# A decoder layer in float32: the second hidden tile of each FFN goes through seven block products

## The chip, the core and the metric

The kernel runs on one core of a Trainium2 chip. The core has a matrix engine (TensorE, PE in the profile, its weight loads PEld), a vector engine (VectorE, DVE), an activation engine (ScalarE, ACT), a general engine (GpSimd, POOL) and a queue engine (SyncE, SP) that issues the DMAs. Each engine works through its own list of instructions in order, and waits on semaphores for the others. The metric is the device time of one execution in microseconds.

## The reference

One layer of a decoder on 1024 tokens of width 1024, all in float32. Two SwiGLU feed-forward networks (FFNs) with a hidden width of 2816 stand at its two ends, and two attentions between them:

```python
def swiglu(x, w_gate, w_up, w_down):
    return (jax.nn.silu(x @ w_gate) * (x @ w_up)) @ w_down

x = x + 0.5 * swiglu(rms_norm(x, ffn1_norm), ffn1_w_gate, ffn1_w_up, ffn1_w_down)
# h = rms_norm(x) @ w_in, two causal attentions, gates, w_o
x = x + 0.5 * swiglu(rms_norm(x, ffn2_norm), ffn2_w_gate, ffn2_w_up, ffn2_w_down)
```

Only `x @ w_gate` and `x @ w_up` of the two FFNs are touched here.

## The kernel before, in words

**Splitting.** Each float32 operand is split into a rounded high part and a rest. ACT casts the high part, DVE subtracts it from the operand (`split_sb`, L157 to L160). A product is then three matmuls: high by high, high by low, low by high.

**Tiles.** The hidden width of 2816 is cut into 22 tiles of 128. Tokens stand in two halves of 512 (n = 0 and 1). For a tile, gate and up have to be computed for both halves of the tokens, over 8 blocks of 128 of the input width.

**A plain tile** takes two outputs, two halves, 8 blocks and 3 matmuls of 128x512: 96 matmuls. In the first FFN tile 0 is begun while the normalisation of the later tokens still runs (`first_half`, L267); the second half of the tokens follows in `ffn_up` (L464). Tile 1 is plain too: its weights are split whole (`col_split`, L434 and L435, 128x1024 each) and `proj_T` does the work (L501 to L506).

**A tile by seven products.** Gate and up, with the input width halved, are the four blocks of a 2x2 matrix, and so are the tokens. Seven products of sums of blocks give the four results (Strassen's scheme in Winograd's form). Each product is 4 blocks of 128 and 3 matmuls, so a tile is 84 matmuls. What it needs beside them:

- the sums of tokens t1 to t4, made once for each FFN (`token_sums`, L533): DVE adds and subtracts whole 128x1024 or 128x2048 pieces (L558, L564, L568, L572, L573), then ACT and DVE split them;
- for each tile the sums of weights, four POOL instructions of 128x512 (`pair_sums`, L596, L597, L598, L609), and seven splits of 128x512 (names `op`), ACT's cast and DVE's subtraction each;
- the adding up in `hidden_tile` (L625): three products share one PSUM bank (`pst`, a), and between them ACT and DVE copy or add what stands in it (L643, L648, L652, L655, L658, L662, L668); the bank may be added to again only when it has been read. The last product of a tile is emitted inside the next tile (`last`, called there as `finish`).

The weights of tile j are loaded two tiles ahead (`pair_load`, L581). The POOL sums of a tile take a buffer of the ring `y`, which has two buffers and is also that of tile 0's two results `a0` (L487). These are written out to DRAM from it (L492).

**Down projection.** `ffn_down` (L675) multiplies by w_down; tiles 2 to 21 go through seven products there as well, from sums that POOL makes of pairs of tiles (`act_sums`, L522). Tiles 0 and 1 are multiplied plainly at its end from `actd`.

**Order.** The order on each engine is set when the program is built, by the order of the Python calls and by the scheduler of the framework; nothing reorders at run time. The stretch that matters here is the beginning of each `ffn_up`: tile 0's second half, the token sums, and tiles 1 and 2.

Of the kernel before, what the change touches and what calls it, by code (L numbers as in the profile page):

```python
# [9 lines left out]
F32 = mybir.dt.float32  # L10
# [3 lines left out]
AF = mybir.ActivationFunctionType  # L14
ALU = mybir.AluOpType
AX = mybir.AxisListType

P = 128
T = 1024
# [4 lines left out]
NH = HID // P  # L24
# [39 lines left out]
class Layer:  # L64
# [399 lines left out]
    def ffn_up(self, norm, name, first, tags):  # L464

        nc = self.nc  # L470
        hi, lo = norm["hi"], norm["lo"]
        hT = hi, lo
        dst, sumd = self.actd[name == "ffn2"], self.sumd[name == "ffn2"]
        sums = norm["ops"]
        even = None
        blocks, (pg, pu) = first
        loads = {j: self.pair_load(name, j, tags["w"]) for j in (2, 3)}
        for n in range(2):
            s = slice(n * HALF, (n + 1) * HALF)
            if n == 1:  # L480
                pg, pu = self.psbg(), self.psbg()
                for o, w in zip((pg, pu), blocks):
                    self.high(o, w, hi[1])
                for o, w in zip((pg, pu), blocks):
                    for f in self.low(o, w, hi[1], lo[1]):
                        f()
            a = self.ring.tile([P, HALF], F32, tag="y", bufs=2, name="a0")  # L487
            nc.scalar.activation(a, pg, AF.Silu)
            if n == 0:
                self.follow(self.last_act)  # L490
            nc.vector.tensor_tensor(out=a, in0=a, in1=pu, op=ALU.mult)
            nc.sync.dma_start(dst[0][:, s], a)  # L492
            sums[1](n)
            if n == 0:
                sums[3](1)
        nxt = self.pair_sums(loads.pop(2))
        sums[2]()
        bg, bu = (self.col_split(l) for l in self.ffn_loads(name, 1))
        sums[4]()
        tok = sums["all"]()  # L500
        pg = self.proj_T(bg, hT)  # L501
        a = self.ring.tile([P, T], F32, tag="y", bufs=2, name="a")
        nc.scalar.activation(a, pg, AF.Silu)
        pu = self.proj_T(bu, hT)
        nc.vector.tensor_tensor(out=a, in0=a, in1=pu, op=ALU.mult)
        nc.sync.dma_start(dst[1], a)  # L506
        ops = [next(nxt) for _ in range(7)]
        finish = None
        for j in range(2, NH):
            if j + 2 < NH:  # L510
                loads[j + 2] = self.pair_load(name, j + 2, tags["w"])
            nxt = self.pair_sums(loads.pop(j + 1)) if j + 1 < NH else iter(())
            e = self.slot(tags["e"][j % 3]).rearrange("p (s n) -> p s n", s=4)
            then = None
            if j % 2:
                then = lambda a=even, b=e, k=j // 2 - 1: self.act_sums(a, b, sumd[:, :, k, :])
            ops, finish = self.hidden_tile(ops, tok, e, nxt, finish, then if j < NH - 1 else None)
            even = e
        finish()
        return then  # L520
# [1075 lines left out]
```

## Time and profile before

| what | value |
|---|---|
| median of 3 runs | 2150.81 us (2148.9 to 2152.93) |
| the profiled execution | 2152.22 us, of it 2150.1 us span from first to last instruction |
| granted TensorE clock | 1.000 |
| PE busy | 2107.7 us (98%) |
| DVE busy | 1323.2 us (62%) |
| ACT busy | 948.4 us (44%) |
| POOL busy | 711.5 us (33%) |

A row of a timeline reads: start in us, duration in us, engine, line, operation, output tile <- input tiles, shapes, count, and in brackets how long the engine was idle before it and what released it. Names leave out buffer numbers: `op` is a split weight operand of the seven products, `s_u`, `s_v`, `s_act`, `s_wd` are the big buffers that hold tokens, weights or results in turn, `psa`, `psb`, `psg`, `pst` are PSUM banks. A row with a count shows the time from the first start to the last end.

### The profile page before, as it was taken

Reading aid. Unit: us, or ns where it says so; the run is one execution under the profiler, and the core shown is the slowest. Engines: PE = TensorE matmul, PEld = TensorE weight load, DVE = VectorE, ACT = ScalarE, POOL = GpSimd, SP = SyncE. Lnnn points to the kernel's source line nnn. Section 1 sums busy time; section 2 is a strip of 40 time slices with the busy share of each in tenths; the row PEclk is TensorE's granted clock in tenths of the full one; section 3 lists DMA queues with packets and bytes.
Section 4 is the critical chain, followed back from the end, with each engine's and each line's share of the span. In section 5 each row is a group of like instructions: output and inputs, shape, how many; then the busy total and the mean of one; then the engine's idle time right before and its main releaser. Section 6 shows DMA issues by size and latency. Waiting matters only on the chain.

```text
span 2150.1 us, 27820 instructions
## 1 busy us (share of the span) xinstructions
PE 2107.7 (98%) x10113; PEld 1758.7 (82%) x10113; DVE 1323.2 (62%) x2140; ACT 948.4 (44%) x1758; POOL 711.5 (33%) x633
## 2 busy tenths in 40 slices
PE   7999999999999989999999999999999999999999
PEld 6888888878888767888888878888888888887887
DVE  7644444467766787645556677753844444449765
ACT  6333333334444544356656765422533333334441
POOL 0565555572201130023333432000354545546200
PEclk9999999999999999999999999999999999999999
DMA  5143332485334376675555774541232434266432
GB/s 172 54 138 98 110 116 89 137 301 173 113 109 148 94 214 194 204 188 138 138 144 139 183 210 126 197 166 65 83 98 79 137 98 135 81 228 239 133 106 107
DMA packets 251633, 305.37 MB, mean 142 GB/s; under 512 B 17656, under 2 KB 186472, under 8 KB 251496
## 3 DMA queue, kind: packets, MB, share of 16 engines
q1 hardware_dynamic: 251496, 303.59, 45.5%
q8 instruction: 80, 1.31, 0.3%
q14 instruction: 57, 0.47, 0.1%
HBM read 205.54 MB, written 98.00 MB: 141 GB/s over the span
## 4 chain that ended last, share of the span: by engine, by line
PE 86%; DVE 4%; issue 3%; DMA 3%; ACT 2%; SPq 1%; POOL 1%; ACTq 0%; POOLq 0%; DVEq 0%
PE pst L620 20%; PE psd L760 16%; PE psb L620 11%; PE psg L620 4%; PE pss L1379 4%; PE pspt L1405 3%; PE pspv L1416 3%; PE psgate L153 2%; PE psgate L155 2%; PE psgate L154 2%; PE psb L153 2%; PE psb L154 2%; PE psb L155 2%; PE psin L153 1%; PE psin L154 1%
## 5 line engine op out<-in xcount | busy, mean ns | idle before, releaser
L760 PE MATMUL psd<-op 128*128 128x512 f32 x1680 | 381.9, 389 | 1.4 <-DVE op L160 1.4
L760 PEld LDWEIGHTS psd<-op 128*128 128x128 f32 x1680 | 315.2, 188 | 67.7 <-DVE op L160 2.3
L160 DVE TENSOR_TENSOR op<-s_u,op 128x512 fp32r<-128x512 f32 x220 | 200.0, 912 | 111.5 <-ACT op L159 111.0
L159 ACT CAST op<-s_u 128x512 fp32r<-128x512 f32 x220 | 136.0, 621 | 214.3 <-PE psd L760 94.1
L620 PE MATMUL pst<-s_u,op 128*128 128x512 f32 x720 | 173.1, 389 | 0.8 <-DVE s_wd L662 0.8
L620 PE MATMUL pst<-s_v,op 128*128 128x512 f32 x640 | 167.9, 389 | 2.8 <-DVE s_u L662 2.8
L160 DVE TENSOR_TENSOR op<-s_act,op 128x512 fp32r<-128x512 f32 x125 | 114.4, 917 | 77.5 <-ACT op L159 77.1
L620 PEld LDWEIGHTS pst<-s_u,op 128*128 128x128 f32 x720 | 135.1, 188 | 29.2 <-DVE s_wd L662 1.2
L620 PEld LDWEIGHTS pst<-s_v,op 128*128 128x128 f32 x640 | 120.1, 188 | 28.2 <-DVE s_u L662 3.3
L1386 ACT ACTIVATE s_act<-pss,nm 128x128 f32<-128x128 f32 (+7 forms) x128 | 94.9, 742 | 100.8 <-DVE nm L1383 100.4
L596 POOL TENSOR_TENSOR sums<-s_u 128x512 f32<-128x512 f32 x20 | 28.0, 1402 | 320.1 <-DVE wlo L435 176.4
L159 ACT CAST op<-s_act 128x512 fp32r<-128x512 f32 x125 | 77.5, 622 | 110.7 <-PE pst L620 55.6
L160 DVE TENSOR_TENSOR op<-sums,op 128x512 fp32r<-128x512 f32 x80 | 60.0, 751 | 86.6 <-ACT op L159 86.1
L1379 PE MATMUL pss<-s_wd 96*128 96x256 f32 (+5 forms) x480 | 112.8, 361 | 0.0
L160 DVE TENSOR_TENSOR op<-s_wd,op 128x512 fp32r<-128x512 f32 x95 | 84.1, 890 | 38.5 <-ACT op L159 38.5
L1424 DVE TENSOR_TENSOR cmb<-pspv,cmb 64x512 f32<-64x512 f32 x64 | 44.1, 688 | 103.5 <-ACT cmb L1423 103.1
L155 PE MATMUL psgate<-s_u,wlo 128*128 128x512 f32 x256 | 100.7, 393 | 1.7 <-POOL wlo L435 1.7
L153 PE MATMUL psgate<-s_u,whi 128*128 128x512 f32 x256 | 101.6, 397 | 0.4 <-ACT z L1228 0.4
L1409 DVE TENSOR_TENSOR s_v<-pspt,s_v 128x512 fp32r<-128x512 f32 (+1 forms) x160 | 96.4, 632 | 7.4 <-ACT s_v L1408 5.8
L154 PE MATMUL psgate<-s_u,whi 128*128 128x512 f32 x256 | 100.7, 393 | 0.0
L159 ACT CAST op<-s_wd 128x512 fp32r<-128x512 f32 x95 | 58.4, 620 | 92.2 <-PE psd L760 89.1
L435 POOL TENSOR_TENSOR wlo<-stg,whi 128x1024 fp32r<-128x1024 f32 x19 | 45.4, 2394 | 160.8 <-DMA mk<-mlo 104.5
(507 smaller groups left out, 4894.0 us busy)
## 6 DMA issues: line engine op xcount, KB each, us to landing
sumd<-s_u SPq DMA_DIRECT2D x20, 1024.0 KB, 4.2
sumd<-s_wd SPq DMA_DIRECT2D x13, 1024.0 KB
s_wd<-fd SPq DMA_DIRECT2D x48, 256.0 KB, 5.4
s_u<-in_ffn_w_down_dram SPq DMA_DIRECT2D x22, 512.0 KB, 6.2
s_wd<-sumd SPq DMA_DIRECT2D x14, 768.0 KB, 4.3
s_u<-sumd SPq DMA_DIRECT2D x14, 768.0 KB, 4.3
s_act<-in_ffn_w_gate_dram SPq DMA_DIRECT2D x20, 512.0 KB, 4.1
s_act<-in_ffn_w_up_dram SPq DMA_DIRECT2D x20, 512.0 KB
```

Source lines behind the costliest of these rows:

```text
L153: mm(out, lhsT=lh, rhs=rh, start=start, stop=False)
L154: mm(out, lhsT=lh, rhs=rl, start=False, stop=False)
L155: mm(out, lhsT=ll, rhs=rh, start=False, stop=stop)
L159: self.nc.scalar.copy(hi, src)
L160: self.nc.vector.tensor_tensor(out=lo, in0=src, in1=hi, op=ALU.subtract)
L620: mm(out, lhsT=a[:, k, :], rhs=b[:, k, :], start=start and k == 0 and i == 0, stop=k == n - 1 and i == 2, skip_group_check=True,)
L760: nc.tensor.matmul(o, lhsT=u[:, r], rhs=w, start=start and m == 0, stop=k == CK - 1 and m == 2, skip_group_check=True,)
L1379: mm(ps[:, b:e], lhsT=a[:, q], rhs=bb[:, b:e], start=k == 0, stop=k == len(passes) - 1)
L1386: nc.scalar.activation(pn[:, :n], ps[:, :n], AF.Exp, bias=nm, accum_out=rs[:, i, j:j + 1])
L1405: nc.tensor.transpose(pt[:, o:o + P], pr[m][:, kt * P:(kt + 1) * P], self.ident)
L1409: nc.vector.tensor_tensor(out=lo, in0=pt[:, s0:], in1=hi, op=ALU.subtract)
L1416: mm(po[:, :256], lhsT=v[:, kt, :], rhs=slabs[c // 2][:, s, c % 2, e * 256:(e + 1) * 256], start=kt == 0 and s == 0, stop=False,)
```

## The change

Tile 1 of each FFN goes through `pair_load`, `pair_sums` and `hidden_tile` as tiles 2 to 21 do, and the plain path for it (two loads, two whole splits, `proj_T`, silu and product) is gone. The weights of tiles 1 and 2 instead of 2 and 3 are loaded ahead, and the calls that split tile 1's weights are put between the calls of the token sums. Tile 1's result is written to `actd` from the tile's result buffer, so that `ffn_down` is as it was. All lines behind the edit stand four lower (L620 is now L616, L658 is L654, L662 is L658).

```diff
         hi, lo = norm["hi"], norm["lo"]
-        hT = hi, lo
         dst, sumd = self.actd[name == "ffn2"], self.sumd[name == "ffn2"]
...
-        loads = {j: self.pair_load(name, j, tags["w"]) for j in (2, 3)}
+        loads = {j: self.pair_load(name, j, tags["w"]) for j in (1, 2)}
...
-        nxt = self.pair_sums(loads.pop(2))
+        nxt = self.pair_sums(loads.pop(1))
+        ops = [next(nxt) for _ in range(2)]
         sums[2]()
-        bg, bu = (self.col_split(l) for l in self.ffn_loads(name, 1))
+        ops += [next(nxt) for _ in range(3)]
         sums[4]()
+        ops += [next(nxt) for _ in range(2)]
         tok = sums["all"]()
-        pg = self.proj_T(bg, hT)
-        a = self.ring.tile([P, T], F32, tag="y", bufs=2, name="a")
-        nc.scalar.activation(a, pg, AF.Silu)
-        pu = self.proj_T(bu, hT)
-        nc.vector.tensor_tensor(out=a, in0=a, in1=pu, op=ALU.mult)
-        nc.sync.dma_start(dst[1], a)
-        ops = [next(nxt) for _ in range(7)]
         finish = None
-        for j in range(2, NH):
+        for j in range(1, NH):
             if j + 2 < NH:
                 loads[j + 2] = self.pair_load(name, j + 2, tags["w"])
             nxt = self.pair_sums(loads.pop(j + 1)) if j + 1 < NH else iter(())
             e = self.slot(tags["e"][j % 3]).rearrange("p (s n) -> p s n", s=4)
             then = None
-            if j % 2:
+            if j == 1:
+                then = lambda e=e: nc.sync.dma_start(dst[1].rearrange("p (s n) -> p s n", s=2), e[:, :2])
+            elif j % 2:
                 then = lambda a=even, b=e, k=j // 2 - 1: self.act_sums(a, b, sumd[:, :, k, :])
```

The order that comes of it, at three places. First TensorE in the first FFN, around the end of tile 0 (L293, L300 and L304 are tile 0). Before:

```order
L304 MATMUL psb<-s_u,whi 128x512 x8
L293 MATMUL psg<-s_u,whi 128x512 x8
L293 MATMUL psb<-s_u,whi 128x512 x8
L300 MATMUL psg<-s_u,wlo 128x512 x8
L304 MATMUL psg<-s_u,whi 128x512 x8
L300 MATMUL psb<-s_u,wlo 128x512 x8
L304 MATMUL psb<-s_u,whi 128x512 x8
L153 MATMUL psa<-s_u,whi 128x512
L154 MATMUL psa<-s_u,whi 128x512
L155 MATMUL psa<-s_u,wlo 128x512
```

and now:

```order
L304 MATMUL psb<-s_u,whi 128x512 x8
L616 MATMUL pst<-s_u,op 128x512 x9
L293 MATMUL psg<-s_u,whi 128x512 x8
L293 MATMUL psb<-s_u,whi 128x512 x8
L300 MATMUL psg<-s_u,wlo 128x512 x8
L304 MATMUL psg<-s_u,whi 128x512 x8
L300 MATMUL psb<-s_u,wlo 128x512 x8
L304 MATMUL psb<-s_u,whi 128x512 x8
L616 MATMUL pst<-s_u,op 128x512 x3
L616 MATMUL psb<-s_u,op 128x512 x12
L616 MATMUL psb<-s_wd,op 128x512 x12
```

The three plain matmuls L153 to L155, which go on 32 times before, are gone. Nine matmuls of tile 1's first product have moved ahead of tile 0's second half, and its second and third product (the third with the token sum t1, in `s_wd`) follow tile 0 at once.

Second TensorE in the first FFN a little later, where tile 1 ends and tile 2 begins; it continues the list above:

```order
L616 MATMUL pst<-s_v,op 128x512 x2
L616 MATMUL pst<-s_u,op 128x512
L616 MATMUL pst<-s_v,op 128x512 x10
L616 MATMUL psb<-s_u,op 128x512 x12
L616 MATMUL pst<-s_wd,op 128x512 x12
L616 MATMUL pst<-s_u,op 128x512 x11
L616 MATMUL psg<-s_u,op 128x512 x12
L616 MATMUL psb<-s_wd,op 128x512 x2
L616 MATMUL pst<-s_v,op 128x512
L616 MATMUL pst<-s_act,op 128x512
```

The last two rows begin tile 1's seventh product, with the token sum t4 (in `s_v` and `s_act`). Ahead of it, 25 matmuls of tile 2 have been placed (`pst<-s_u` x11, `psg<-s_u` x12, `psb<-s_wd` x2; one more `pst<-s_u` stands earlier). In the second FFN the same place reads as follows; there 16 matmuls of tile 2 (`pst<-s_act`, `psb<-s_act` x4) stand ahead of the seventh product, which is `pst<-s_u`:

```order
L616 MATMUL psb<-s_v,op 128x512 x12
L616 MATMUL pst<-s_u,op 128x512 x12
L616 MATMUL psb<-s_wd,op 128x512 x12
L616 MATMUL pst<-s_v,op 128x512 x12
L616 MATMUL pst<-s_act,op 128x512 x12
L616 MATMUL psb<-s_act,op 128x512 x4
L616 MATMUL pst<-s_u,op 128x512 x12
```

Third VectorE in the first FFN, from the second result of tile 0 on (L491, now L490). Before, up to the split of t4 (`s_act<-s_v`):

```order
L491 TENSOR_TENSOR a_505<-a_505,psb 128x512
L160 TENSOR_TENSOR s_wd<-s_v,s_wd 128x4x256
L435 TENSOR_TENSOR wlo<-stg,whi 128x1024
L160 TENSOR_TENSOR s_v<-s_v 128x2048
L160 TENSOR_TENSOR op<-s_act,op 128x512
L572 TENSOR_TENSOR s_v<-s_u,s_v 128x2048
L573 TENSOR_TENSOR s_v<-s_v,s_u 128x2048
L160 TENSOR_TENSOR op<-s_act,op 128x512 x2
L160 TENSOR_TENSOR s_act<-s_v 128x2048
```

and now, from the subtraction for t4 (L569) to the reading of tile 1's shared bank (L658):

```order
L569 TENSOR_TENSOR s_v<-s_v,s_u 128x2048
L160 TENSOR_TENSOR op<-s_act,op 128x512 x2
L644 TENSOR_TENSOR s_u<-psb,s_u 128x512
L160 TENSOR_TENSOR op<-s_act,op 128x512
L160 TENSOR_TENSOR s_act<-s_v 128x2048
L160 TENSOR_TENSOR op<-s_act,op 128x512
L160 TENSOR_TENSOR op<-sums,op 128x512
L654 TENSOR_TENSOR s_u<-psb,s_u 128x512
L160 TENSOR_TENSOR op<-s_act,op 128x512
L658 TENSOR_TENSOR s_u<-pst,s_u 128x512
```

Between the first L490 and this L658 there are now 16 DVE instructions on 128x512, 5 on 128x1024 and 5 on 128x2048, in either FFN. From the first L491 to the split of t4 there were before 5 on 128x512 (4 in the second FFN), 7 on 128x1024 and 5 on 128x2048. L658 now stands behind the split of t4 and three splits of tile 2; the seventh product adds to the bank that it reads.

## The prediction

> **What bounds the kernel now.** I read the page first (busy shares, the chain), then the busy time by stretch around the edit, then the timelines of PE, DVE and POOL in that stretch.
>
> ```profile
> span 2150.1 us, 27820 instructions
> PE 2107.7 (98%) x10113; PEld 1758.7 (82%) x10113; DVE 1323.2 (62%) x2140; ACT 948.4 (44%) x1758; POOL 711.5 (33%) x633
> PE 86%; DVE 4%; issue 3%; DMA 3%; ACT 2%; SPq 1%; POOL 1%; ACTq 0%; POOLq 0%; DVEq 0%
> ```
>
> Over the whole run PE is the bound: it is busy 98% of the span and 86% of the chain that ended last. That is an average, though. The next rows are three stretches: tile 1 of the first FFN, tile 2 of the first FFN, tile 1 of the second FFN. Columns are the length, then busy us (and instructions) of PE, PEld, DVE, ACT, POOL, then clock and DMA.
>
> ```profile
> 51.30:73.10 21.80, 21.80 (x98) 18.04 (x97) 20.64 (x14) 8.76 (x11) 9.42 (x4) 1.00 0.22 61
> 73.10:92.10 19.00, 19.00 (x85) 15.75 (x84) 10.51 (x12) 7.55 (x13) 11.98 (x8) 1.00 0.07 29
> 1527.20:1549.00 21.80, 21.80 (x98) 18.04 (x97) 20.21 (x14) 8.60 (x11) 9.33 (x4) 1.00 0.21 61
> ```
>
> PE has no gap in any of them, at full clock. But while the plain tile runs, DVE is busy 20.64 of 21.80 us, and 20.21 in the second FFN; one tile later it is half idle. So the plain tile is the cover under which DVE makes the token sums. The edit shortens that cover and puts more splits under it. ACT (8.76 of 21.80) has room.
>
> **PE's side of the change.**
>
> ```profile
> 40.28 2.12 PE L293 MATMUL psg<-s_u,whi 128*128 128x512 f32 x8 [0.89 <-ACT s_u L408]
> ...
> 51.32 0.39 PE L153 MATMUL psa<-s_u,whi 128*128 128x512 f32 x1
> ...
> 73.08 2.88 PE L620 MATMUL pst<-s_u,op 128*128 128x512 f32 x12
> ...
> 92.12 0.39 PE L620 MATMUL pst<-s_v,op 128*128 128x512 f32 x1
> ...
> 1527.21 0.39 PE L153 MATMUL psa<-s_act,whi 128*128 128x512 f32 x1
> ...
> 1548.97 2.88 PE L620 MATMUL pst<-s_act,op 128*128 128x512 f32 x12
> ```
>
> The plain tile takes 73.08 - 51.32 = 21.76 us for 96 matmuls, 0.2267 us each. A tile of seven products takes 92.12 - 73.08 = 19.04 us for 84, the same 0.2267. So each FFN saves 12 matmuls, 2.72 us, and both 5.44 us, if PE never waits. In the first FFN nine matmuls of tile 1 (2.04 us) also move ahead of the 40.28 row, where PE idled 0.89 us; tile 0 then ends at most 2.04 - 0.89 = 1.15 us later, at 52.5, and 2.04 us of tile 1 are done. That is 0.89 us more. Nothing else is lost or won on PE itself: -3.61 us in the first FFN, -2.72 in the second.
>
> **DVE and POOL.** These decide. First their prices, from the same stretch:
>
> ```profile
> 44.44 0.69 DVE L491 TENSOR_TENSOR a<-a,psb 128x512 f32<-128x512 f32 x1
> 45.04 1.22 DVE L160 TENSOR_TENSOR s_wd<-s_v,s_wd 128x1024 fp32r<-128x1024 f32 x1
> 46.18 1.22 DVE L160 TENSOR_TENSOR s_wd<-t,s_wd 128x1024 fp32r<-128x1024 f32 x1
> ...
> 50.84 2.29 DVE L568 TENSOR_TENSOR s_v<-s_v 128x2048 f32<-128x2048 f32 x1
> 53.04 0.68 DVE L491 TENSOR_TENSOR a<-a,psb 128x512 f32<-128x512 f32 x1
> ...
> 55.91 2.29 DVE L160 TENSOR_TENSOR s_v<-s_v 128x2048 fp32r<-128x2048 f32 x1
> 58.11 1.78 DVE L160 TENSOR_TENSOR op<-s_act,op 128x512 fp32r<-128x512 f32 x1
> 59.82 3.38 DVE L572 TENSOR_TENSOR s_v<-s_u,s_v 128x2048 f32<-128x2048 f32 x1
> 63.23 3.27 DVE L573 TENSOR_TENSOR s_v<-s_v,s_u 128x2048 f32<-128x2048 f32 x1
> ...
> 68.54 2.47 DVE L160 TENSOR_TENSOR s_act<-s_v 128x2048 fp32r<-128x2048 f32 x1 [0.84 <-ACT s_v L159]
> 70.93 0.68 DVE L160 TENSOR_TENSOR op<-sums,op 128x512 fp32r<-128x512 f32 x1
> 71.54 1.28 DVE L160 TENSOR_TENSOR op<-s_act,op 128x512 fp32r<-128x512 f32 x2
> ...
> 1519.95 0.68 DVE L491 TENSOR_TENSOR a<-a,psg 128x512 f32<-128x512 f32 x1
> ...
> 1544.12 2.29 DVE L160 TENSOR_TENSOR s_u<-s_u 128x2048 fp32r<-128x2048 f32 x1 [1.38 <-ACT s_u L159]
> ```
>
> ```profile
> 56.38 2.96 POOL L596 TENSOR_TENSOR sums<-s_act 128x512 f32<-128x512 f32 x1 [54.08 <-DMA actd<-a]
> 59.42 1.62 POOL L597 TENSOR_TENSOR s_act<-s_act 128x512 f32<-128x512 f32 x1
> 61.13 3.22 POOL L598 TENSOR_TENSOR sums<-s_act 128x512 f32<-128x512 f32 x1
> 67.24 1.61 POOL L609 TENSOR_TENSOR s_act<-s_act,sums 128x512 f32<-128x512 f32 x1 [2.90 <-DVE op L160]
> ```
>
> From start to start, DVE needs 0.61 us for 128x512 (70.93 to 71.54), 1.14 for 128x1024 (45.04 to 46.18), 2.20 for 128x2048 (50.84 to 53.04). From 58.11 on, where POOL works too, each takes about 1.1 us longer: 1.78 instead of 0.69, 3.38 and 3.27 instead of 2.29. POOL is stretched in turn. Its L598 begins at 61.13, while L572 runs until 63.20, and ends at 64.35, 1.15 us after that; L573, begun at 63.23, ends at 66.50, 2.15 us after L598. The two take turns, whole instructions at a time. So a POOL sum costs DVE 1.15 us.
>
> [...]
>
> ```profile
> 78.72 0.69 DVE L648 TENSOR_TENSOR s_act<-psb,s_act 128x512 f32<-128x512 f32 x1
> 79.42 1.06 DVE L160 TENSOR_TENSOR op<-s_act,op 128x512 fp32r<-128x512 f32 x1
> ...
> 78.30 1.63 POOL L598 TENSOR_TENSOR sums<-s_act 128x512 f32<-128x512 f32 x1
> ```
>
> L648, which reads PSUM, took its bare 0.69 us beside POOL's 78.30 to 79.93; the split behind it was held until then.
>
> The prices are tried on the kernel before. From 44.44 to the end of the split of t4 DVE does 5 x 0.61 + 7 x 1.14 + 5 x 2.20 = 22.03 us, POOL's four sums 4.60: 26.63, that is 71.07. The trace has 68.54 + 2.47 = 71.01. In the second FFN, with one 128x512 less, 26.02 from 1519.95 give 1545.97, and the trace has 1546.41. So the sum of both engines' work, laid end to end, tells when DVE is done to 0.5 us, small waits included. PE did not notice: it took t4 up at 92.12.
>
> **Where the new order puts the wait.** Tile 1's seventh product adds to the bank that L658 reads, and in DVE's queue L658 stands behind the split of t4 and three of tile 2's splits. From the first L490 to L658 there are 16 x 0.61 + 5 x 1.14 + 5 x 2.20 = 26.46 us of DVE. POOL has to run four sums for tile 1 and four for tile 2 in that time (DVE splits all of them), and the next tile's first stands right behind: 9 x 1.15 = 10.35. Together 36.8 us. One split (0.61) has also moved ahead of L490 in the first FFN.
>
> First FFN: 44.44 + 0.61 + 36.81 = 81.9. PE's turn for the seventh product comes 89 matmuls (20.18 us) after tile 0's end at 52.5: 72.7. It waits 9.2 us (earlier waits for t1 or the splits of POOL's sums are part of this). Net 9.2 - 3.6 = +5.6 us. Second FFN: 1519.95 + 36.81 = 1556.8; the turn comes 88 matmuls (19.95 us) after 1527.2, at 1547.15. It waits 9.6 us: net +6.9. Together +12.5 us. For holes in the DVE queue (ACT's casts now wait on POOL, and t1's second cast is queued behind two such casts on ACT) I add 0.4 us per FFN, what the second FFN showed above: +13.3 us.
>
> Lower end: all five PSUM readers of each FFN (L490 twice, L644, L654, L658) lie beside POOL, no hole: 12.5 - 6.1 = +6.4. Upper end: every instruction at its full duration rather than from start to start (0.08 us more for each of 26, 0.15 for each of 9) adds 3.4 per FFN: +19.3. I take the value near the middle, since the same prices met the kernel before to 0.5 us.
>
> **What costs nothing.** The loads: pair loads of tile 1 take the place of tile 2's, far ahead of their use, and two plain loads go.
>
> ```profile
> 11.75 0.43 SPq L586 DMA_DIRECT2D s_act<-in_ffn_w_gate_dram  x1
> ...
> s_act<-in_ffn_w_gate_dram SPq DMA_DIRECT2D x20, 512.0 KB, 4.1
> ```
>
> Issued from 11.75 on and landed 4.1 us later, they are there before the first split; without that lead tile 1 would start up to 4.1 us late. The write of tile 1's result waits for its last product; behind it on SP stand loads that are wanted two tiles later, and only the end of `ffn_down` reads what it writes. After tile 2 DVE has 19.00 - 10.51 us to spare per tile, so the backlog ends there; but PE, busy without a gap, cannot win back what it waited.
>
> **Rivals.**
> 1. POOL's sums fit beside DVE, and the saving shows. Then DVE alone decides: 44.44 + 0.61 + 26.46 = 71.5, before 72.7, and 1546.4, before 1547.15. No wait: -6.3 us, 2144.5. For it: PE is the bound nearly everywhere. Against it: the 1.78 and 3.38 us rows. Chance 0.06.
> 2. POOL's sums for tile 1 run before the crowd. In the first FFN POOL was free until 56.38 and waited for the buffer of tile 0's result; if tile 1's four sums find a free buffer before 44.44, 4 x 1.15 = 4.6 us leave each sum: 13.3 - 9.2 = +4.1, 2154.9, at the edge of what can be told. Against it: the ring `y` has two buffers, which tile 0's results take. Chance 0.08.
> 3. The backlog reaches tile 3: the late seventh product also delays POOL's product of tile 1 and the next sums, and PE waits once more, by one more set of four sums (4.6 us) per FFN: +22.5, 2173.3. Against it: DVE's 8.5 us to spare in tile 2. Chance 0.08.
>
> The forecast itself has 0.78.
>
> **How the numbers follow.** Against the profiled execution (2152.2, of it 2150.1 span) the sum gives 2165.5. The median of the runs shown is 1.4 us below that execution, so the predicted median is 2150.8 + 13.3 = 2164.1. The range from +6.4 to +19.3 is 2157.2 to 2170.1; the ends need all unknowns on one side, and I take 2157 to 2170. It leaves out the first and third rival and most of the second. A measurement of this kernel tells about 0.2%, 4.3 us, from no change. Faster by more: 0.06 (the first rival). Within: 0.06, most of the second. Slower: 0.88.
>
> **What would show it.** In the changed kernel's trace: PE idle of 8 to 11 us in all between tile 0 and tile 3 of each FFN, the largest piece ahead of the `pst` product with t4 and released by DVE's L658; this L658 near 81 to 83 us; DVE without gaps from 44 to 82; POOL's sums at 1.6 to 3.3 us each there; tile 3 onwards without gaps as before. It is wrong if POOL's sums take 1.3 us beside busy DVE, if L658 comes before 75 us, or if PE has no gap there.

## The result

The changed kernel takes 2164.1 us in the median (2162.5 to 2165.5) against 2150.8 us before: a ratio of 1.0057, 95% interval 1.0046 to 1.0068, that is 9.9 to 14.6 us slower. The profiled execution took 2163.95 us, 2162.1 us of it span.

The page of the changed kernel: span, busy time by engine, and the chain that ended last.

```profile
span 2162.1 us, 27835 instructions
PE 2111.9 (98%) x10089; PEld 1759.1 (81%) x10089; DVE 1340.5 (62%) x2156; ACT 955.8 (44%) x1776; POOL 736.0 (34%) x643
PE 84%; DVE 6%; issue 4%; DMA 2%; ACT 2%; SPq 1%; POOL 1%; ACTq 0%; DVEq 0%; POOLq 0%
```

PE has 24 matmuls fewer (10089 for 10113), and is busy 4.2 us longer all the same. DVE's share of the chain rose from 4% to 6%, PE's fell from 86% to 84%: somewhere PE now waits for DVE. The page does not say where. The stretches do; in the row of a stretch PE's busy time stands behind the length, then PEld, DVE, ACT, POOL, and the clock is the third number from the end.

```profile
54.70:76.50 21.80, 18.51 (x71) 13.95 (x70) 19.62 (x15) 12.47 (x18) 11.22 (x7) 0.92 0.31 89
...
1546.00:1560.80 14.80, 9.71 (x40) 7.35 (x40) 14.80 (x14) 6.49 (x11) 7.05 (x3) 0.92 0.26 71
1560.80:1566.00 5.20, 5.16 (x14) 4.14 (x15) 3.98 (x4) 0.48 (x2) 5.00 (x4) 0.58 0.31 90
1566.00:1581.00 15.00, 15.00 (x68) 12.43 (x67) 8.40 (x10) 5.85 (x10) 9.29 (x7) 1.00 0.24 75
```

Where PE was busy 21.80 of 21.80 us before, it is busy 18.51 now. In the second FFN DVE works without a pause (14.80 of 14.80) while PE has work for 9.71 us. Then comes something new: 5.2 us in which PE is busy throughout at a granted clock of 0.58. From 1566 on all is as before.

PE's timeline shows what it waits for (start, duration, line, operands, count, and in brackets the idle time ahead of the row and its releaser), in the first FFN from the end of tile 0 and then in the second up to tile 3:

```profile
54.73 0.84 PE L616 MATMUL pst<-s_u,op 128*128 128x512 f32 x3
...
59.46 3.19 PE L616 MATMUL psb<-s_wd,op 128*128 128x512 f32 x11 [0.93 <-DVE s_wd L160]
...
64.16 0.50 PE L616 MATMUL pst<-s_v,op 128*128 128x512 f32 x1 [1.29 <-DVE s_v L160]
...
65.85 3.92 PE L616 MATMUL pst<-s_v,op 128*128 128x512 f32 x10 [0.96 <-DVE op L160]
...
82.74 0.47 PE L616 MATMUL pst<-s_v,op 128*128 128x512 f32 x1 [1.64 <-DVE s_u L658]
...
98.71 0.39 PE L616 MATMUL pst<-s_v,op 128*128 128x512 f32 x1
...
1531.73 2.88 PE L616 MATMUL pst<-s_act,op 128*128 128x512 f32 x12
...
1539.28 2.81 PE L616 MATMUL psb<-s_v,op 128*128 128x512 f32 x11 [1.72 <-DVE s_v L160]
...
1546.07 3.03 PE L616 MATMUL psb<-s_wd,op 128*128 128x512 f32 x12 [1.21 <-ACT s_wd L648]
...
1560.84 5.00 PE L616 MATMUL pst<-s_u,op 128*128 128x512 f32 x12 [4.79 <-DVE s_wd L658]
1565.68 1.98 PE L616 MATMUL psb<-s_act,op 128*128 128x512 f32 x8
...
1581.09 2.88 PE L616 MATMUL pst<-s_u,op 128*128 128x512 f32 x12
```

The waits are small ones for token sums and operands, and a last one ahead of tile 1's seventh product, which L658 releases in both FFNs. In all PE is idle for 4.8 us in the first FFN and for 8.0 in the second (0.27 of it not shown). And two rows are slow once they have begun: 10 matmuls from 65.85 on take 3.72 us from start to start for work of 2.27, and the 12 of the seventh product, from 1560.84 to 1565.68, take 4.84 us for work of 2.72.

DVE (first seven rows) and POOL (last three) in the same stretches:

```profile
45.84 0.68 DVE L490 TENSOR_TENSOR a<-a,psb 128x512 f32<-128x512 f32 x1
...
53.79 3.37 DVE L564 TENSOR_TENSOR s_v<-s_v 128x2048 f32<-128x2048 f32 x1
57.09 0.68 DVE L490 TENSOR_TENSOR a<-a,psb 128x512 f32<-128x512 f32 x1
...
64.02 1.77 DVE L160 TENSOR_TENSOR op<-sums,op 128x512 fp32r<-128x512 f32 x1
...
81.92 0.68 DVE L658 TENSOR_TENSOR s_u<-pst,s_u 128x512 f32<-128x512 f32 x1
...
1524.49 0.68 DVE L490 TENSOR_TENSOR a<-a,psb 128x512 f32<-128x512 f32 x1
...
1560.02 0.68 DVE L658 TENSOR_TENSOR s_wd<-pst,s_wd 128x512 f32<-128x512 f32 x1
...
48.71 2.38 POOL L592 TENSOR_TENSOR sums<-s_act 128x512 f32<-128x512 f32 x1 [46.40 <-DMA actd<-a]
...
55.09 3.23 POOL L605 TENSOR_TENSOR s_act<-s_act,sums 128x512 f32<-128x512 f32 x1
...
75.04 1.31 POOL L605 TENSOR_TENSOR s_act<-s_act,sums 128x512 f32<-128x512 f32 x1 [8.10 <-DVE op L160]
```

From the first L490 to the end of L658 it is 82.60 - 45.84 = 36.8 us in the first FFN and 1560.70 - 1524.49 = 36.2 in the second. Beside POOL's sums DVE's instructions are 1.1 us longer again (3.37, 1.77). POOL's sums take 1.6 to 3.4 us there (2.38 and 3.23 are shown); the one at 75.04, which begins while DVE stands idle, takes 1.31. The second L490, which reads PSUM, takes its bare 0.68 us at 57.09, while POOL's row of 55.09 still runs.

**A measure for what follows.** In either FFN I take the time from tile 0's end to a fixed row at tile 3 (54.73 to 98.71, 1531.73 to 1581.09 here) and subtract what its matmuls need at 0.2267 us each: 159 of them, 36.04 us, in the first FFN, 168, 38.08 us, in the second. What is left is PE's loss, waiting and slow clock together: 43.98 - 36.04 = 7.9 us and 49.36 - 38.08 = 11.3 us. The kernel before loses nothing here (40.80 us for 180 matmuls in both), but has more to do; the change saves 3.61 and 2.72 us by the prediction's count, 6.3 together, so a kernel's expected time is about 2150.8 - 6.3 + its two losses. The measure does not see what PE loses ahead of tile 0's end, or anywhere else.

### The profile page after: what moved, and what is told of

It reads as the page before. It is cut to its first block, busy times and chain, and to the rows that moved or that the text cites. A ratio compares the mean times of both kernels' runs of the same rounds, so it can differ in the third digit from the quotient of the medians.

```text
span 2162.1 us, 27835 instructions
## 1 busy us (share of the span) xinstructions
PE 2111.9 (98%) x10089; PEld 1759.1 (81%) x10089; DVE 1340.5 (62%) x2156; ACT 955.8 (44%) x1776; POOL 736.0 (34%) x643
## 3 DMA queue, kind: packets, MB, share of 16 engines
q8 instruction: 79, 1.29, 0.2%
## 4 chain that ended last, share of the span: by engine, by line
PE 84%; DVE 6%; issue 4%; DMA 2%; ACT 2%; SPq 1%; POOL 1%; ACTq 0%; DVEq 0%; POOLq 0%
PE pst L616 20%; PE psd L756 16%; PE psb L616 11%; PE psg L616 4%; PE pss L1375 4%; PE pspt L1401 3%; PE psgate L153 3%; PE psgate L155 3%; PE psgate L154 3%; PE pspv L1412 3%; PE psb L153 2%; PE psb L155 2%; PE psb L154 2%; DVE op L160 2%; PE psin L153 1%
## 5 line engine op out<-in xcount | busy, mean ns | idle before, releaser
L160 DVE TENSOR_TENSOR op<-s_u,op 128x512 fp32r<-128x512 f32 x225 | 205.1, 914 | 111.4 <-ACT op L159 110.8
L616 PE MATMUL pst<-s_u,op 128*128 128x512 f32 x756 | 184.3, 393 | 5.6 <-DVE s_wd L658 5.6
L616 PE MATMUL pst<-s_v,op 128*128 128x512 f32 x672 | 179.6, 394 | 7.0 <-DVE s_u L658 4.5
L616 PEld LDWEIGHTS pst<-s_u,op 128*128 128x128 f32 x756 | 143.2, 190 | 36.4 <-ACT s_u L639 5.2
L160 DVE TENSOR_TENSOR op<-s_act,op 128x512 fp32r<-128x512 f32 x130 | 123.3, 950 | 73.4 <-ACT op L159 72.9
L616 PEld LDWEIGHTS pst<-s_v,op 128*128 128x128 f32 x672 | 127.5, 190 | 35.6 <-DVE s_u L658 3.3
L160 DVE TENSOR_TENSOR op<-sums,op 128x512 fp32r<-128x512 f32 x84 | 67.6, 805 | 84.4 <-ACT op L159 83.9
L153 PE MATMUL psgate<-s_u,whi 128*128 128x512 f32 x256 | 101.7, 397 | 0.1
L155 PE MATMUL psgate<-s_u,wlo 128*128 128x512 f32 x256 | 100.6, 393 | 0.0
```

Of the source, the lines that this page charges most:

```text
L153: mm(out, lhsT=lh, rhs=rh, start=start, stop=False)
L155: mm(out, lhsT=ll, rhs=rh, start=False, stop=stop)
L160: self.nc.vector.tensor_tensor(out=lo, in0=src, in1=hi, op=ALU.subtract)
L616: mm(out, lhsT=a[:, k, :], rhs=b[:, k, :], start=start and k == 0 and i == 0, stop=k == n - 1 and i == 2, skip_group_check=True,)
```

## The experiments

A summary first; each follows with its text on record. Losses come from one profiled execution each, the time is the median. In e7 and e9 the 18 unread matmuls (4.1 us) count as loss of the second FFN.

| kernel | loss, first FFN | loss, second FFN | 2144.5 + both | median us |
|---|---|---|---|---|
| the change | 7.9 | 11.3 | 2163.7 | 2164.1 |
| the change, run again (e11) | 8.7 | 12.0 | 2165.2 | 2163.9 |
| tiles 1, 2 without POOL's sums (e3) | 0.0 | 0.0 | 2144.5 | 2144.2 |
| POOL's sums made, not used (e4) | 7.5 | 7.5 | 2159.5 | 2157.9 |
| tile 1's sums on DVE (e5) | 7.0 | 4.3 | 2155.8 | 2155.4 |
| tiles 1, 2's sums on DVE (e10) | 6.9 | 4.9 | 2156.3 | 2155.3 |
| tile 1's sums early (e6) | 9.3 | 4.0 | 2157.8 | 2160.9 |
| tile 2's splits behind L658 (e8) | 10.1 | 8.1 | 2162.7 | 2163.0 |
| 18 unread matmuls, same bank (e7) | 8.7 | 15.3 | 2168.5 | 2165.5 |
| 18 unread matmuls, other bank (e9) | 8.7 | 10.2 | 2163.4 | 2160.9 |

The measured median meets the sum in the fourth column within 1.6 us but for three rows: e6 is 3.1 us above it, e7 and e9 are 3.0 and 2.5 us below. Executions of one kernel lie 3 to 10 us apart (2162.5 to 2165.5 for the change, 2150.8 to 2160.9 for e2 further down), so I read nothing from differences below 3 us between these two columns. The kernel before, measured again beside each group, had medians of 2150.9 to 2151.6.

### The change once more

The same program, to see which rows come again (its file has one line more at the head, so L659 in it is L658 above).

> The changed kernel once more, beside the two above, to see what of its trace comes again: the wait of 4.8 us ahead of the seventh product in the second FFN with 12 products of 4.84 us behind it, and 49.4 us from the first hidden product there to tile 3. By the theory both follow from the order of the instructions and come again within a few tenths; if they are chance of one execution, they move by microseconds. Time 2162 to 2166.

2163.9 us (2162.3 to 2167.5), 1.0064 [1.0052, 1.0077]. PE's timeline, and below it the stretches:

```profile
52.06 0.84 PE L617 MATMUL pst<-s_u,op 128*128 128x512 f32 x3
...
58.28 4.70 PE L617 MATMUL psb<-s_wd,op 128*128 128x512 f32 x11 [1.74 <-DVE s_wd L161]
...
80.80 0.47 PE L617 MATMUL pst<-s_v,op 128*128 128x512 f32 x1 [2.43 <-DVE s_u L659]
...
1529.28 2.88 PE L617 MATMUL pst<-s_act,op 128*128 128x512 f32 x12
...
1558.40 5.46 PE L617 MATMUL pst<-s_u,op 128*128 128x512 f32 x12 [4.81 <-DVE s_wd L659]
```

```profile
30.00:51.00 21.00, 18.01 (x90) 14.77 (x89) 20.10 (x26) 14.41 (x25) 3.36 (x2) 1.00 0.07 14
...
1558.40:1564.00 5.60, 5.60 (x13) 4.42 (x14) 3.92 (x4) 0.41 (x2) 5.44 (x4) 0.50 0.38 112
```

In the second FFN the waits came again to 0.1 us (4.81 ahead of the seventh product), and the slow matmuls came again a little slower (5.26 us from start to start instead of 4.84). In the first FFN the sum of the waits is 5.6 instead of 4.8 us and the slow matmuls lie in another place (11 from 58.28 on, in 4.5 us). Tile 0's end came at 52.06 instead of 54.73: from 30 to 51 us the execution profiled first had a clock of 0.84, this one 1.00. (The first 30 us do not decide it: there e9 further down had 0.83, as the execution profiled first, and with 1.00 behind them tile 0's end at 51.93.) So 2.7 us of the earlier trace's lateness there are chance, and do not belong to the change.

### Each FFN alone

> The change in the first FFN alone; the second FFN as before. Theory (VectorE and GpSimd take turns at one port, and their queued work makes TensorE wait at tile 1's seventh product in each FFN by itself): the first FFN's part of the trace of the change, +4.5 to +6.5 us, so 2155.3 to 2157.3 us against 2150.8. Rival (the loss comes from one of the two FFNs alone, the second with its long wait): 2147 to 2151, the saving of this FFN or nothing.

> The change in the second FFN alone. Theory: +6.9 us by the sum of the prediction, +8.6 with the slow TensorE clock behind the wait of 4.8 us that the trace shows, so 2157.7 to 2159.4 us. Both single changes together should give the whole loss of 13.3 us. Rival (loss in the first FFN alone): 2148 to 2151.

The other FFN calls the function of the kernel before, kept as `ffn_up_plain`:

```diff
-pending = self.ffn_up(norm2, "ffn2", first, tags)          # e1; in e2 the call for "ffn1"
+pending = self.ffn_up_plain(norm2, "ffn2", first, tags)
```

2155.2 us, 1.0021 [1.0010, 1.0031], with the change in the first FFN alone, and 2155.4 us, 1.0018 [1.0006, 1.0029], in the second alone: the first 0.1 us, the second 2.3 us below the range that I had put on record. By the measure above the losses are 9.5 us and 8.9 us. The second is 2.4 to 3.1 us less than in the whole change: with the first FFN's code exchanged, PE's queue had another order there (two matmuls of tile 1 ahead of tile 0's second half, one product in another bank), and the long wait ahead of the seventh product did not form:

```profile
1537.39 0.50 PE L674 MATMUL pst<-s_u,op 128*128 128x512 f32 x1 [1.96 <-DVE s_u L160]
1539.07 4.63 PE L674 MATMUL pst<-s_u,op 128*128 128x512 f32 x10 [1.17 <-DVE op L160]
...
1554.14 2.99 PE L674 MATMUL pst<-s_u,op 128*128 128x512 f32 x12 [0.49 <-DVE s_wd L716]
```

So both FFNs lose time, each more than it saves. That the two medians, 3.6 and 3.8 us above the kernel before, add to 7.5 us and not to 13 is partly this, and partly within their intervals (2.2 to 6.7 and 1.3 to 6.2 us). The traces show one more part, outside the two FFNs: from the first to the last `pspt` matmul of the attentions, which no run changes, PE needed 418.0 us in the profiled execution of the kernel before, 416.3 in e1, 415.7 in e2 and 416.2 in the change, but 417.8 in e10 further down. With one trace of the kernel before it stays open whether these 2 us are the kernel or that execution.

### Without POOL's sums, and with sums that nobody uses

In e3 the four pair sums of tiles 1 and 2 are left out in both FFNs (DVE splits unsummed weights instead), so POOL does nothing in the crowd. In e4 they are left out too, but POOL makes four subtractions per tile whose result nobody reads.

```diff
+if mode:
+    if mode == 'free':                 # e4 alone
+        for _ in range(4):
+            pool(out=s3, in0=a11, in1=a12, op=ALU.subtract)
+    s3 = s2 = a22
+    pool = lambda **k: None
```

> The change with the GpSimd sums of the weights of tiles 1 and 2 left out in both FFNs; the splits take unsummed weights, so the results of these two tiles are not those of the reference. Takes away both the port's use and the waits for GpSimd's results. Theory: VectorE alone needs 26.5 us, TensorE hardly waits, the whole saving of 6.3 us shows: 2144 to 2147 us. Rival (VectorE's own queue or ScalarE's casts are the cause, GpSimd is not): 2160 to 2164.

> As the run without GpSimd's sums, but GpSimd does four subtractions of 128x512 for each of tiles 1 and 2 into a buffer that nobody reads; the splits take unsummed weights, so these tiles' results are not the reference's. No instruction waits for GpSimd's results, only the port is shared. Theory (the port): 8 x 1.15 = 9.2 us per FFN are back in VectorE's queue: 2158 to 2164 us. Rival (what cost the time was that splits waited for GpSimd's results, the port does not matter): as without the sums, 2144 to 2147.

e3: 2144.2 us, 0.9966 [0.9955, 0.9978]. e4: 2157.9 us, 1.0037 [1.0023, 1.0052]. DVE's timeline in the first FFN, without the sums:

```profile
52.88 2.29 DVE L564 TENSOR_TENSOR s_v<-s_v 128x2048 f32<-128x2048 f32 x1
...
73.03 0.68 DVE L664 TENSOR_TENSOR s_u<-pst,s_u 128x512 f32<-128x512 f32 x1
```

and DVE and POOL with the unused ones:

```profile
57.49 3.37 DVE L160 TENSOR_TENSOR s_v<-s_v 128x2048 fp32r<-128x2048 f32 x1
60.78 1.77 DVE L160 TENSOR_TENSOR op<-s_act,op 128x512 fp32r<-128x512 f32 x1
62.48 3.36 DVE L568 TENSOR_TENSOR s_v<-s_u,s_v 128x2048 f32<-128x2048 f32 x1
...
47.87 24.10 POOL L595 TENSOR_TENSOR sums<-s_act 128x512 f32<-128x512 f32 x8 [45.57 <-DMA actd<-a]
```

Without the sums every DVE instruction of this stretch has its bare duration (0.68 to 0.69, 1.22 and 2.29 us), the last update of tile 1's bank (L664 here) starts at 73.03 instead of 81.92, PE has no gap, and the whole 6.3 us of saving come out: 2144.2 where the prediction's first rival, which let the sums cost nothing, had 2144.5. Sums without a reader bring 13.8 of the 20 us back. Nothing waits for them, and PE has the same order of matmuls in e3 and e4, so what they cost, they cost DVE through its own longer instructions (1.77, 3.36 and 3.37 us above, bare 0.68 and 2.29). What the two engines share there, the port of these expectations, is my assumption: the runs show the turns, not what is behind them. The price per sum was lower than the prediction's 1.15 us, though: from the first L490 (45.00) to the end of L664 (78.93) it is 33.9 us in the first FFN here, 7.5 above DVE's own 26.46, so 0.93 us for each of the eight, and the time is 0.1 us below the range on record. The other 6 us of the change are then the order that true sums force (splits that wait for them, casts behind those on ACT); that is the remainder, not a measurement of its own.

### The sums on DVE

```diff
-nxt = self.pair_sums(loads.pop(1))
+nxt = self.pair_sums(loads.pop(1), nc.vector)     # e5: tile 1; e10: tile 2 too
```

> The four pair sums of tile 1 go to VectorE in both FFNs; POOL keeps those of tile 2. Theory (VectorE and POOL take turns at SBUF, a POOL sum costs VectorE 1.15 us): each of the four sums now costs the shared queue 0.61 instead of 1.15, 4 x 0.54 = 2.2 us less per FFN, 4.3 us in all: 2157 to 2161 us. Rival (the limit is VectorE's own queue, POOL runs beside it for nothing): four more instructions of 0.61 us in that queue, +2.4 per FFN: 2167 to 2170 us.

> The pair sums of tiles 1 and 2 go to VectorE in both FFNs, POOL has none of them in the crowded stretch. Theory (turns at SBUF): the prediction's shared queue of 26.46 + 9 x 1.15 = 36.8 us becomes 26.46 + 9 x 0.61 = 31.9, 4.9 less per FFN, and with the sums of tile 2 in VectorE's order only as they are needed perhaps more: 2152 to 2157 us. Rival (POOL runs beside VectorE for nothing and the limit is VectorE's own queue): 8 instructions more of 0.61 in that queue, +4.9 per FFN: 2170 to 2175.

e5: 2155.4 us, 1.0021 [1.0013, 1.0030]; e10: 2155.3 us, 1.0020 [1.0011, 1.0029]. Giving the busy engine four or eight more instructions makes the kernel 9 us faster. The rival (DVE's own queue is the limit, POOL is free beside it) asked for 2167 to 2175 and is dead. In e5 the stretch from the first L490 to the end of L658 is 34.6 us in the first FFN and 33.5 in the second (44.53 to 79.12, 1522.27 to 1555.73), where the change had 36.8 and 36.2: shorter by 2.2 and 2.7 for a predicted 2.2, though DVE does more. PE at tile 1's third product in the first FFN and at its seventh in the second:

```profile
60.21 5.49 PE L616 MATMUL psb<-s_wd,op 128*128 128x512 f32 x12 [3.73 <-ACT op L159]
...
1555.88 2.98 PE L616 MATMUL pst<-s_u,op 128*128 128x512 f32 x12 [1.01 <-DVE s_wd L658]
```

The gain of time is larger than my 2157 to 2161, and the second FFN says why: 10 matmuls more stand ahead of this product in PE's new order (2.3 us of work for the wait), and behind a wait of only 1.01 us the 12 took 2.82 us for work of 2.72. These two make up the rest of the 7 us by which the loss fell there, so part of this gain came with a new order of PE and not with the shorter stretch. In the first FFN the wait ahead of the seventh product is gone too, but the loss is still 7.0 us: PE waits 3.73 us for an operand of the third product, and the 12 matmuls behind that wait take 5.28 us instead of 2.72.

e10 brought nothing more than e5, though its four further sums were to give another 2.2 us per FFN. Its stretches are 36.0 and 33.9 us, not 31.9. POOL did not stay away: with nothing else to do it took up tile 3's sums in the crowd, and the wait of PE moved to tile 2's second product (3.25 and 2.96 us), whose splits now stand behind tile 2's own sums on DVE. One row of POOL is of use further down, with the DVE row during which it ended:

```profile
63.47 9.28 POOL L592 TENSOR_TENSOR sums<-s_act 128x512 f32<-128x512 f32 x1 [61.17 <-PE psb L616]
...
71.52 0.68 DVE L644 TENSOR_TENSOR s_u<-psb,s_u 128x512 f32<-128x512 f32 x1
```

### The sums early

A buffer of its own for tile 1's sums, so that POOL need not wait until tile 0's result has been written from the shared ring.

```diff
-nxt = self.pair_sums(loads.pop(1))
+own = self.slot(tags["w"])[:, :1024].rearrange("p (a k n) -> p a k n", a=2, k=4)
+nxt = self.pair_sums(loads.pop(1), own)
```

> Tile 1's pair sums get a buffer of their own instead of that of tile 0's activations, so that they need not wait until the write of tile 0 has read it. This is the mechanism of the prediction's second rival, made to happen. If POOL's four sums of tile 1 leave the crowd in both FFNs, the price of the prediction gives 4 x 1.15 x 2 = 9.2 us less than 2164: 2154 to 2156 us. If tile 2's sums move up into the place that becomes free, as POOL then has nothing else to do, or the weights land too late in the second FFN, less: 2157 to 2162. If the sums do not matter where they lie (the rival: the data dependency alone makes the wait): 2164.

2160.9 us, 1.0043 [1.0029, 1.0056]. Three of the four sums did move out of the crowd (to 23 us, and to 1514 in the second FFN), and the second FFN's loss fell from 11.3 to 4.0 us. The first FFN's rose to 9.3. POOL, ACT and PE there:

```profile
48.12 6.91 POOL L594 TENSOR_TENSOR sums<-s_act 128x512 f32<-128x512 f32 x1 [19.89 <-DMA actd<-a]
...
58.93 1.25 POOL L607 TENSOR_TENSOR s_act<-s_act 128x512 f32<-128x512 f32 x1
...
60.22 0.62 ACT L159 CAST op<-s_act 128x512 fp32r<-128x512 f32 x1 [6.77 <-POOL s_act L607]
...
63.69 0.80 PE L618 MATMUL pst<-s_v,op 128*128 128x512 f32 x1 [4.55 <-ACT s_v L159]
```

Tile 2's three sums went ahead of tile 1's fourth (L607) on POOL. ACT's cast of that fourth operand waited for it 6.77 us at the head of ACT's queue, and behind it stood the cast of a token sum that PE needed: a wait of 4.55 us. In the second FFN the early sums also lie beside the norm's DVE work, and a wait of PE for it grew from 0.75 to 1.72 us; this lies ahead of tile 0's end, so the loss in the table does not hold it. So the place of the sums matters, as the second rival had it, but what leaves the crowd is replaced by what POOL does next.

### Tile 2's splits behind L658

```diff
 def prep(n=1):
+    if late and n == 1:      # tile 1 only: most of tile 2's splits are written
+        return               # after the seventh product's update
...
+if late:                     # behind L658 in the order of the calls
+    for _ in range(2):
+        prep(2)
 prep()
...
+for _ in range(5 if late else 0):      # at the end of last()
+    prep(2)
 prep()
```

> Tile 2's splits are written behind tile 1's seventh product, so VectorE does the last update of tile 1 (the one that ended at 82.6 us in the first FFN) ahead of six of them, by VectorE's prices 5 x 1.27 + 2.20 = up to 8 us earlier. If the wait of TensorE is only the order of VectorE's queue, the wait ahead of the seventh product goes and tile 2 takes its operands as they come: 2154 to 2158 us. If the sum of VectorE's and POOL's work between the first token sum and tile 2 is what decides (the prediction's theory), the wait only moves from tile 1's end to tile 2's first products, and the time stays: 2162 to 2166 us.

2163.0 us, 1.0057 [1.0043, 1.0070]: no gain. PE in the second FFN:

```profile
1556.07 3.00 PE L616 MATMUL pst<-s_u,op 128*128 128x512 f32 x12 [0.93 <-DVE s_wd L660]
...
1569.40 3.01 PE L616 MATMUL psg<-s_wd,op 128*128 128x512 f32 x12 [2.17 <-ACT s_u L650]
...
1577.69 2.88 PE L616 MATMUL pst<-s_u,op 128*128 128x512 f32 x12
```

The wait ahead of the seventh product shrank from 4.79 to 0.93 us, as the other reading had it, and a new one of 2.17 us stands in tile 2. The loss in this FFN fell by 3 us (no long idle time in one piece; the 12 matmuls behind these two waits took 2.84 and 2.85 us from start to start), and rose by 1.4 to 2.2 us in the first, where tile 2 waited twice (1.14 and 1.42 us). So here the sum of the work decided, not the place of L658 in DVE's queue.

### Is it the idle time that slows the clock?

18 matmuls that nobody reads, ahead of the seventh product in the second FFN: in e7 into the unused half of tile 1's own accumulator, in e9 into a bank whose last reader was long done.

```diff
 def last():
+    for i in range(fill):                        # 18, second FFN, tile 1
+        nc.tensor.matmul(spare, lhsT=ops[5][0][:, i % 4, :],   # e9: b for spare
+                         rhs=tok[5][0][:, i % 4, :], ...)
     step(6, a, False)
```

> 18 matmuls whose result nobody reads stand ahead of the seventh product of tile 1 in the second FFN alone, where TensorE waited 4.79 us in the trace of the changed kernel; at 0.2267 us they take 4.1 us and end before that wait does. If the idle time itself lowers the granted clock behind it (12 products then took 4.84 us instead of 2.72, clock 0.58), this gives some 2 us back and the clock of that stretch stays near 1.0: 2161 to 2163 us in the median, the stage of the second FFN 2 us shorter in the trace. If the clock falls for another reason: 2164, and the slow stretch stays.

> As in the run before with the 18 unread matmuls ahead of the seventh product of tile 1 in the second FFN, but into another bank of PSUM: in that run they went into the second half of tile 1's own accumulator and so waited themselves for the same update of VectorE (4.69 us), ran at the low clock in its place (18 took 6.22 us instead of 4.08), and the 12 products behind them took 2.72. Now nothing holds them: they should run in the wait. If an idle TensorE is what lowers the clock, the 12 products behind the wait take 2.72 to 3.0 us instead of 4.84 and the stretch from the first hidden product of the second FFN to tile 3 (49.4 us in the trace of the changed kernel, 53.4 in that run) takes 47 to 48 us; total 2161 to 2163. If the clock falls for another reason, 49.4 again, and 2164.

e7: 2165.5 us, 1.0068 [1.0054, 1.0081]. It missed its aim: the unread matmuls themselves waited for L658 (L659 there), which reads the other half of the same tile.

```profile
1556.27 6.38 PE L665 MATMUL pst<-s_v,op 128*128 128x512 f32 x18 [4.69 <-DVE s_wd L659]
1562.49 2.89 PE L616 MATMUL pst<-s_u,op 128*128 128x512 f32 x12
```

They took the low clock in the place of the seventh product (6.22 us instead of 4.08), whose 12 matmuls behind them ran in 2.72. In e9 they ran in the wait:

```profile
1552.49 4.24 PE L664 MATMUL psb<-s_v,op 128*128 128x512 f32 x18
1558.40 3.00 PE L616 MATMUL pst<-s_u,op 128*128 128x512 f32 x12 [1.67 <-DVE s_wd L658]
```

The seventh product started as long after tile 0's end as without them (29.2 us), and its 12 matmuls took 2.84 us instead of 4.84 and 5.26. So it is the idle time: 4.8 us of it cost another 2.1 to 2.5 us afterwards. The stretch took 48.3 us, at the slow end of what I expected and beyond it by 0.3: four matmuls of tile 2 that used to stand ahead of the wait (0.9 us) had moved behind it. The time, 2160.9 us, 1.0055 [1.0040, 1.0070], is 3 us below the change run beside it, but the two intervals overlap: it is the trace that shows this, not the median.

## Why the prediction was right

**PE's saving.** Predicted 3.61 + 2.72 us if PE never waits. The kernel without POOL's sums shows it: 2144.2 us for a predicted 2144.5, and 7.4 us (interval 4.7 to 9.7) below the kernel before that was measured beside it.

**DVE's and POOL's sum.** Predicted 36.8 us from the first L490 to the end of L658, in both FFNs. Measured 36.8 and 36.2, and 36.0 and 36.2 when run again. The price of 1.15 us for a POOL sum was the heart of it, and the experiments that remove the sums, make them useless, or move them to DVE all have the sign that it gives. e3 against e4 is the cost of the sums: 13.8 us for 16 of them and the waits that follow. The lower end of the range took off 3.05 us per FFN (6.1 in both) for five PSUM readers that cost nothing beside POOL. No run shows this term: L490 at 57.09 took its bare 0.68 us beside a POOL sum, but the measured sums are at most 0.9 us below the one without it.

The size of the price was less good than its sign. In the second FFN, where DVE has no gap, the nine sums made DVE's part longer by 9.7 us, 1.08 each; in the first FFN of e4 it was 0.93 each. In the first FFN DVE's busy time grew by 7.8 us only, 0.87 each, and 2.5 us of gaps, which the sum leaves out, filled the rest; POOL was at work for 1.8 us of them. So the agreement to 0.1 us in the first FFN is partly luck.

**The wait at the seventh product.** Predicted 9.2 and 9.6 us behind PE's turn. In the second execution of the change, whose clock was 1.00 up to 51 us, PE's turn was 52.06 + 20.18 = 72.2 (predicted 72.7) and the product came at 80.80: 8.6 us. In the first it was 54.73 + 20.18 = 74.9 and 82.74: 7.8 us. In the second FFN the turn was 19.95 us after tile 0's end, and the product came 9.2 us later in both executions. These include, as the prediction said, the earlier waits for token sums.

**What the steps missed.** "PE idle of 8 to 11 us in all between tile 0 and tile 3" was wrong in the first FFN: only 4.8 and 5.6 us there are idle, and 3.1 us more are lost to slow matmuls; the second FFN has 8.0 us of idle time and 3.3 to 4.0 of slow matmuls. The prediction had no term for the clock. Where the slow matmuls come before L658's release, they cost nothing more, since PE would have waited that time (first FFN: 8.6 us of lateness become 8.7). Where they come after it, they add up: 2.1 and 2.8 us in the second FFN. This took the place of the 0.4 us per FFN for holes in DVE's queue, a term that came from the wrong mechanism, and of the 0.4 us (second FFN) and 0.6 to 1.4 us (first) by which the two waits came out shorter. So the sum was 13.3 and the losses of the two executions give 12.9 and 14.3 (19.2 and 20.6 less 6.3): the right total, with the second FFN at +8.6 to +9.3 instead of +7.3, and the first at +4.3 to +5.0 instead of +6.0. The way to the wait was right; that the median came out at the predicted 2164.1 to the tenth is luck, as two errors of 1 to 2 us with opposite signs cancel in it.

**"DVE without gaps from 44 to 82"** was nearly so: in the execution profiled first there are gaps of 1.8, 0.4 and 0.3 us in the first FFN and none in the second. The 1.8 us (for a cast on ACT that stood behind casts waiting for POOL) is the hole that the 0.4 us stood for. It did not make the sum longer, as POOL ran a sum of tile 2 in 1.25 us of it. Tile 3 onwards ran without gaps beyond those of the kernel before, as predicted.

**The rivals.** The first (sums cost nothing) and the condition named for it fell at once: POOL's sums took 1.6 to 3.4 us beside busy DVE. The second (sums ahead of the crowd) did not happen, for the reason given, the ring's buffers: POOL's first sum waited for the write of tile 0's result until 48.71. Made to happen, it gave 9.9 us over before, not 4.1, as tile 2's sums moved up. The third (backlog in tile 3) did not happen.

## What to carry over

When an engine off the critical path is almost fully busy under a cover, and work is added under a shorter cover, lay the work of all engines that take turns end to end from a fixed event to the instruction that releases the bound engine, and compare with that engine's turn: here it gave the release to 0.9 us in 36.8, though with a price per sum that was too high (1.15 us against 0.87 to 1.08) and with gaps that it left out. Then price the wait itself with what comes behind it: idle time of PE ahead of matmuls that are on the path also cost up to 2.8 us of slow matmuls. If such a cover is too short, moving helper work from POOL, with which it takes turns, to the busy DVE (0.61 us instead of 1.15) helped more than either reordering of the helper work that was tried (2155.4 against 2160.9 and 2163.0 us), though no version that computes the layer beat the kernel before.

## What was not expected of the hardware

- **The clock after a wait.** After 4.8 us without work PE's granted clock was 0.50 to 0.58 for the next 5 us and 12 matmuls took 4.84 to 5.26 us instead of 2.72; with 18 unread matmuls in that wait, 2.84. While the clock was 0.50 a matmul took 0.43 us instead of 0.23; the clock was 1.00 again 4.3 us after the wait's end in the first execution and 5.7 us in the second. The length of one wait did not decide it in these runs. In the first FFN of the second execution waits of 0.42 and 1.74 us with one matmul between them stood ahead of 11 matmuls that took 4.5 us instead of 2.5; in the first execution, before the slow matmuls of the row from 65.85, it was 0.93, 1.29 and 0.96 us with work between. And in e10 ten matmuls behind a wait of 2.96 us in the second FFN took 3.90 us from start to start, but ten behind one of 3.25 us in the first took 2.40. What decides between such cases was not tested.
- **Turns are not always one for one.** The prediction said that DVE and POOL take turns, whole instructions at a time. In e10 the POOL sum begun at 63.47 lasted 9.28 us, while seven DVE instructions on two SBUF operands each took their bare durations (0.68, 2.28); it ended at 72.75, 1.2 us after DVE began L644, which reads PSUM (71.52). The second FFN of e10 has the same (6.86 us, ended 1.2 us after L644), and so have e6 (6.91 us, ended 1.2 us after L490) and one sum of the change run again (4.42 us from 73.86, ended 1.2 us after L655, which is L654 above). In the first FFN of e4 the unused sums began at 47.87, and no DVE instruction was longer than bare until the one behind L490 (53.55). So a POOL sum can be passed over several times; each of the four with a duration above ended 1.2 us after DVE began an instruction that reads PSUM. In the execution of the change that was profiled first (POOL's sums took 1.6 to 3.4 us beside busy DVE), and for the seven other sums of e4's first FFN (seven DVE instructions there took 1.07 to 1.10 us longer), the turns were one for one. What decides between the two was not tested. A sum that was passed over cost DVE less than the 1.15 us of the prediction: in e10 the DVE instruction behind L644 took 2.78 us instead of 2.28, in e4 the one behind L490 took 1.72 instead of 1.22.
